# A hybrid decoder layer on one core: 32 of 152 attention steps turned by TensorE, and a written order for every engine in that stage

## The chip, the cores and the metric

The kernel runs on one core of one Trainium2 chip. The metric is the device time of one execution, in microseconds (us). The engines are TensorE (PE, with its weight load PEld), VectorE (DVE), ScalarE (ACT), GpSimd (POOL) and SyncE (SP). Before the change SP issues all DMAs. Each engine works through its own instructions in order, and waits where an operand is not ready.

## The reference, cut to what matters

```
a = rmsnorm(x, g_in)                                   # 2048 rows, 1024 wide
q, k, v, gate_b, u, v_a, gate_a = split(a @ w_in)      # 7 pieces of 512 columns
q, k = rope(rmsnorm(q)), rope(rmsnorm(k))              # 8 heads of 64
for (window, r) in ((128, 1), (512, 4), (2048, 16)):   # three dilated branches
    each block of 128 queries attends to its own and the previous 128 keys of its class
merge the three by their softmax denominators          # o_b
u, v_a = gelu(u), layernorm(gelu(v_a))                 # gMLP, chunks of 128 rows
o_a = u * (tril(w_spatial) @ v_a + b_spatial)          # 4 groups, 128 x 128 weights
h = x + [o_b * silu(gate_b), o_a * silu(gate_a)] @ w_out
out = h + sigmoid(rmsnorm(h) @ w_ple_gate + b) * (p @ w_ple_proj)
```

## The kernel before, in words

All large products are made of float32 words split in two parts, so a product of 128 rows by 512 columns is 24 matmuls (`project`, L223; `gm_product`, L640). Rows are worked in 16 tiles of 128.

Stage 1 computes q, k, v and gate_b tile by tile and writes them to DRAM (`d_qk`, `d_vp`, `d_vt`, `d_gb`). At its end PE's order is written by hand: g of tiles 14 and 15, q of both, k14, `spatial_weights` (L467), k15, v14, v15. `spatial_weights` masks the four 128 x 128 triangles on DVE (L476) and turns them on PE (L477); it needs the constants that `gm_constants` (L458) loads. In the same place three more groups of `w_in` columns (`va`, `ua`, `ga`) are loaded in pieces of 256 KB through four staging tiles named `raw` (L127), split by ACT (L133) and DVE or POOL (L135), and the first three quarters of q and k come back from DRAM (`load_qk`, L258).

Stage 2 is attention and gMLP together. Attention is a plan of 152 steps. A step has up to four segments of 128 or 256 keys. `scores` (L762) makes them on PE in a PSUM bank (`s` twice, `av` once in turn, L766), DVE adds the mask and takes the minimum (L773) and shifts it (L779), ACT takes the exponent (L781). `turn` (L784), one step later, makes two float16 words (ACT L788, POOL L789, which shows as L114), and one DMA transpose turns both (L792). `values` (L798), six steps after the scores, multiplies with v. Between `turn` and `values` PE gets a piece of gMLP: `fill(1.3)` (L821) takes some six of the 24 matmuls of a product. `gelu2` (L630), `gm_v`, `gm_u` and `gm_g` hold what follows such a product on ACT, DVE and POOL. Twelve groups of steps ("quads") make one pair of heads; the q and k of the next pair are loaded from the last quads of the pair before on (L848).

In stage 2 only PE's order is written (`manual_schedule(engines={PE})`, L533). The order of ACT, DVE, POOL and SP comes from the tile framework, which sets it from its own estimate of when each instruction can run.

Stage 3 (L866 on) finishes the last three gMLP chunks (`tail`), merges the branches, and does the output projection and the gate.

Of the kernel before, what the change touches and what calls it, by code (L numbers as in the profile page):

```python
# [10 lines left out]
F32 = mybir.dt.float32  # L11
F32R = mybir.dt.float32r
F16 = mybir.dt.float16
# [68 lines left out]
def hybrid_layer(ctx: ExitStack, tc: tile.TileContext, io, out):  # L82
# [11 lines left out]
    d_qk = [dram.tile([128, HEADS, S], F16, name=f"d_{n}") for n in "qk"]  # L94
# [151 lines left out]
    def gm_rows(c, pool):  # L246

        if c < NT and c not in GT:
            if c + 1 < NT:
                XT[c + 1] = load_x(d_at[c + 1])  # L250
            xt, aT = XT.pop(c), rows_T(pool)
            split_words(two(xt), aT)
            GT[c] = aT
# [4 lines left out]
    def load_qk(qk, hp, c, n=1):  # L258

        tl = slice(512 * c, 512 * (c + n))  # L260
        for h in range(2):
            nc.sync.dma_start(qk[0][h][:, tl], d_qk[0][:, 2 * hp + h, tl])
            yield
        for i in (0, 64):
            for t in range(2):
                nc.sync.dma_start(qk[1][i:i + 64, t, :, tl], d_qk[1][64 * t:64 * t + 64, 2 * hp:2 * hp + 2, tl])
            yield

    gating, s2 = ExitStack(), ExitStack()
    with ExitStack() as s1, ExitStack() as s1q:  # L270
# [156 lines left out]
        def turn_qk(n, which, hl):  # L427
# [8 lines left out]
            nc.sync.dma_start(d_qk[which][:, :, n * 128:(n + 1) * 128], st)  # L436
# [21 lines left out]
        def gm_constants():  # L458
            for name, src in (("lng", bcast(io["ln_v_g"], 512)), ("lnb", bcast(io["ln_v_b"], 512)),
# [5 lines left out]
                nc.sync.dma_start(dst if name != "gg" else dst.rearrange("p (g s) -> p g s", g=4), src)  # L465

        def spatial_weights():  # L467

            wsT, gg, bs = pg.tile([128, 4, 128], F32, name="wsT"), CG["gg"], CG["bs"]
            CG["wsT"] = wsT  # L470
            keep = stage()[:, 0:128]
            nc.vector.tensor_scalar(keep, CG["mask"][:, 384:512], 0.0, None, op0=OP.is_ge)
            pt = bank("pt", (128, 4, 128))
            for g in range(4):
                w = gg[:, g * 128:(g + 1) * 128]
                last = nc.vector.scalar_tensor_tensor(w, w, 0.25, keep, op0=OP.mult, op1=OP.mult)  # L476
                nc.tensor.transpose(pt[:, g], w, ident)  # L477
            nc.vector.tensor_copy(wsT, pt)
            with tc.issue_after(last.ins):
                nc.vector.tensor_scalar(bs, bs, 0.25, None, op0=OP.mult)  # L480
# [53 lines left out]
        for n in (NT - 2, NT - 1):  # L534
# [4 lines left out]
        qk = ([p2.tile([128, S], F16, name="sq" + n) for n in "01"],  # L539
              p2.tile([128, 2, 2, S], F16, name="sk"))  # L540
        gm_constants()
# [7 lines left out]
        load_gm("va", 5)  # L549
        for q in range(3):  # L550
            for _ in load_qk(qk, 0, q):
                pass
        step(NT - 2, "k")
        spatial_weights()
        step(NT - 1, "k")
        load_gm("ua", 4)
        step(NT - 2, "v")
# [66 lines left out]
    with s2:  # L624
# [4 lines left out]

        def gelu2(c, ps, name):  # L630
# [3 lines left out]
            nc.scalar.activation(t, ps, AF.Square, scale=math.sqrt(0.044715))  # L634
            nc.vector.scalar_tensor_tensor(t, t, 1.0, ps, op0=OP.add, op1=OP.mult)
            nc.scalar.activation(t, t, AF.Tanh, scale=math.sqrt(2 / math.pi))
            nc.vector.scalar_tensor_tensor(t, t, 1.0, ps, op0=OP.add, op1=OP.mult)  # L637
# [17 lines left out]
        def gm_v(c):  # L655
            ps = yield from gm_product(c, "va", {12: lambda: gm_rows(c + 1, stream)})
            t = gelu2(c, ps, "gv")
            st = small.tile([128, 6], F32, name="st")
            nc.vector.bn_stats(st, t)
            mv = small.tile([128, 2], F32, name="mv", bufs=2)  # L660
            nc.vector.bn_aggr(mv, st)
            rs = small.tile([128, 1], F32, name="rsl")
            rms_scale(rs, mv[:, 1:2], 1.0, 1, 4 * EPS)
            nc.vector.tensor_scalar(t, t, mv[:, 0:1], rs, op0=OP.subtract, op1=OP.mult)
            pool_tt(t, t, lng, OP.mult)
            pool_tt(t, t, lnb, OP.add)
# [5 lines left out]

        def gm_g(c):
            ps = yield from gm_product(c, "ga")
            GT.pop(c)
            t = pg.tile([128, 512], F32, name="gg")
            nc.scalar.activation(t, ps, AF.Tanh, scale=0.5)
# [291 lines left out]
```

## Time and profile before

| what | value |
| --- | --- |
| three runs | 1299.02, 1300.75 (median), 1304.36 us |
| profiled execution, its own time | 1296.61 us |
| its span, first to last instruction | 1294.8 us |
| busy share of the span: PE, DVE, ACT, POOL | 93%, 68%, 50%, 40% |
| mean granted TensorE clock | 0.979 of full speed |

A row of the timeline has the start, the length, the engine, the line, the operation, what is written from what, and how many instructions were merged; in brackets is the idle time before it and what ended that. A row of the stretches has the busy time of each engine, then the clock granted to PE (1.00 is full speed, 2.4 GHz), the mean share of the 16 DMA engines and GB/s. In the trace, the first attention scores start at 414.97 us and the last values end at 817.3 us.

### The profile page before, as it was taken

How to read it: one execution, taken by the hardware profiler on the slowest of the kernel's cores; microseconds unless marked ns; L12 is line 12 of the kernel's file. 1: busy time of each engine (PE TensorE's matmuls, PEld its weight loads, DVE VectorE, ACT ScalarE, POOL GpSimd, SP SyncE). 2: the span in 40 equal slices, each digit the busy share in tenths (PEclk: the TensorE clock that was granted, in tenths of full speed). 3: DMA queues.
4: the chain of work that ended last, by engine and by line, in shares of the span. 5: the costliest groups of instructions: out<-in, count | busy, mean ns of one | idle time of the engine just before them, and what ended most of it. 6: DMA issues, size and time to landing. Idle time of an engine off the chain costs nothing.

```text
span 1294.8 us, 21315 instructions
## 1 busy us (share of the span) xinstructions
PE 1198.9 (93%) x7166; PEld 972.6 (75%) x7166; DVE 878.0 (68%) x2253; ACT 647.6 (50%) x1273; POOL 516.2 (40%) x454
## 2 busy tenths in 40 slices
PE   5999999989949899899899899799999999999998
PEld 4778877777837687687687687677778888888887
DVE  5885665656546878678688679578866776666733
ACT  5754334343324677677677677144434434434422
POOL 4852444434334566556556556331312112121100
PEclk9999999999979999899999999899999999999999
DMA  7598776777679899999999999645454555654531
GB/s 260 160 230 199 178 185 155 167 181 179 163 198 241 198 207 220 220 233 222 222 222 222 221 226 211 179 135 186 119 168 119 156 168 131 153 159 127 143 90 49
DMA packets 442254, 233.21 MB, mean 180 GB/s; under 512 B 337440, under 2 KB 392864, under 8 KB 442144
## 3 DMA queue, kind: packets, MB, share of 16 engines
q1 hardware_dynamic: 442144, 231.85, 74.5%
q8 instruction: 56, 0.92, 0.3%
q14 instruction: 54, 0.44, 0.1%
HBM read 102.66 MB, written 57.28 MB: 124 GB/s over the span
## 4 chain that ended last, share of the span: by engine, by line
PE 40%; DMA 21%; DVE 14%; issue 7%; ACT 7%; POOL 6%; SPq 4%; DVEq 0%; ACTq 0%; POOLq 0%
PE mm L227 17%; PE mm L646 8%; PE gt L227 5%; DMA pt<-raw 4%; DMA st<-hl 4%; PE s L227 3%; DMA xt<-raw 3%; PE s L770 2%; PE pt L806 2%; DMA sk<-d_k 2%; ACT raw L179 2%; DVE aT L194 2%; DVE pr L773 2%; DVE m L421 1%; POOL rsh L148 1%
## 5 line engine op out<-in xcount | busy, mean ns | idle before, releaser
L227 PE MATMUL mm<-wslot,aT 128*128 128x512 f32 x1536 | 361.6, 391 | 5.8 <-ACT wslot L133 3.3
L227 PEld LDWEIGHTS mm<-wslot,aT 128*128 128x128 f32 x1536 | 288.5, 188 | 68.4 <-ACT wslot L133 4.6
L646 PE MATMUL mm<-wslot,aT 128*128 128x512 f32 x1152 | 312.5, 412 | 2.9 <-DVE gv L637 2.4
L646 PEld LDWEIGHTS mm<-wslot,aT 128*128 128x128 f32 x1152 | 210.1, 194 | 42.0 <-DVE gv L637 3.0
L114 POOL TENSOR_TENSOR raw<-pr,raw 128x512 f16<-128x512 f32 (+1 forms) x152 | 178.9, 1183 | 136.2 <-ACT raw L788 114.1
L781 ACT ACTIVATE pr<-pr,ost 128x256 f32<-128x256 f32 (+1 forms) x384 | 150.3, 451 | 67.4 <-DVE ost L779 66.3
L227 PE MATMUL gt<-wslot,aT 128*128 128x512 f32 x744 | 179.0, 395 | 4.0 <-DVE gb L453 3.5
L227 PEld LDWEIGHTS gt<-wslot,aT 128*128 128x128 f32 x744 | 140.7, 190 | 36.6 <-DVE gb L453 5.2
L806 PEld LDWEIGHTS <-pt 128*128 128x128 f16 x1800 | 65.2, 98 | 65.2 <-DMA pt<-raw 32.6
L788 ACT ACTIVATE raw<-pr 128x512 f16<-128x512 f32 (+1 forms) x152 | 93.0, 619 | 34.9 <-DMA pt<-raw 32.9
L806 PE MATMUL pt<-sv,pt 128*128 128x65 f16 x1800 | 83.1, 195 | 24.5 <-DMA pt<-raw 23.3
L773 DVE CUSTOM_DVE_ANT_0 pr<-s,mask 128x256 f32<-128x256 f32 (+1 forms) x256 | 80.9, 360 | 24.6 <-POOL raw L114 11.8
L227 PE MATMUL s<-wslot,aT 128*128 128x512 f32 x384 | 91.9, 395 | 1.4 <-POOL wslot L135 1.4
L227 PE MATMUL av<-wslot,aT 128*128 128x512 f32 x360 | 86.8, 395 | 6.3 <-DVE gb L453 5.3
L114 POOL TENSOR_TENSOR m<-m,m 128x512 f32<-128x512 f32 x32 | 48.1, 1503 | 98.5 <-DVE rsh L147 92.6
L227 PEld LDWEIGHTS s<-wslot,aT 128*128 128x128 f32 x384 | 73.2, 191 | 17.2 <-POOL wslot L135 1.8
L227 PEld LDWEIGHTS av<-wslot,aT 128*128 128x128 f32 x360 | 67.5, 189 | 22.8 <-DVE gb L453 7.0
L770 PEld LDWEIGHTS <-sq 128*128 128x128 f16 x768 | 70.3, 121 | 16.7 <-issue 12.8
L582 POOL TENSOR_TENSOR ob<-ob 128x512 f32<-128x512 f32 x16 | 21.0, 1310 | 143.3 <-DVE ob L580 143.3
L770 PE MATMUL s<-sk,sq 128*128 128x256 f16 (+1 forms) x512 | 73.7, 279 | 4.1 <-DMA sk<-d_k 2.0
L585 POOL TENSOR_TENSOR ma<-ob,ma 128x512 f32<-128x512 f32 x16 | 23.7, 1483 | 121.7 <-DMA ma<-d_gb 86.4
L779 DVE TENSOR_SCALAR ost<-ost 128x2 f32<-128x2 f32 (+1 forms) x152 | 63.1, 417 | 2.3
(198 smaller groups left out, 1722.1 us busy)
## 6 DMA issues: line engine op xcount, KB each, us to landing
xt<-x SPq DMA_DIRECT2D x32, 512.0 KB, 4.4
d_o<-ost SPq DMA_DIRECT2D x48, 264.0 KB, 3.5
raw<-w_in SPq DMA_DIRECT2D x38, 256.0 KB, 3.8
sv<-d_vt SPq DMA_DIRECT2D x32, 264.0 KB, 3.6
ob<-d_o SPq DMA_DIRECT2D x16, 528.0 KB, 4.5
xt<-d_at SPq DMA_DIRECT2D x16, 512.0 KB, 4.4
out<-th SPq DMA_DIRECT2D x32, 256.0 KB, 2.7
d_at<-raw SPq DMA_DIRECT2D x28, 256.0 KB, 2.5
```

What stands on the lines that cost most here:

```text
L114: nc.gpsimd.tensor_tensor(dst, a, b, op=op)
L179: nc.scalar.activation(turned[t].bitcast(U16), words[:, t], AF.Copy)
L194: nc.vector.tensor_tensor(lo, f, hi.bitcast(F32), op=OP.subtract)
L227: nc.tensor.matmul(ps, aT[:, ha, k, :], w(slot, hw, k), start=(n == 0), stop=(n == 3 * nk - 1))
L585: nc.gpsimd.tensor_tensor(m, o, m, op=OP.mult)
L646: nc.tensor.matmul(ps, GT[c][:, ha, k, :], slots[g][:, hw, k, :], start=(n == 0), stop=(n == 23))
L770: nc.tensor.matmul(ps[:, c:c + nk], cols(br, j, Q[h]), cols(br, j, K, n, h, self.nb), start=(n == 0), stop=(n == 1))
L773: nc.vector.tensor_tensor_reduce(pr[:, c:c + nk], ps[:, c:c + nk], mask[:, m - nk:m], -1.0, 3e38, op0=OP.add, op1=OP.min, accum_out=o[:, j ...
L779: nc.vector.tensor_scalar(nm, nm, math.log(PSCALE), None, op0=OP.add)
L781: nc.scalar.activation(pr[:, c:c + nk], pr[:, c:c + nk], AF.Exp, bias=o[:, j - j0, 130 + h:131 + h], scale=-1.0)
L788: nc.scalar.activation(ph, pr[:, :width], AF.Copy)
L806: nc.tensor.matmul(PO[0][:, j % 2, h], self.pt[:, t, c // 128], vt[:, h, vv, 0:65], start=(n == 0), stop=(n == 3 * self.nb - 1))
```

## The change

Names are as in the code above. What is changed:

- The triangles are masked later (`spatial_scales`), and turned on PE (`spatial_weights`) only when the first `gm_g` starts, inside stage 2.
- The constants, and the first three quarters of q and k, are issued by ACT. q and k in DRAM are laid out by quarters, so that a quarter is three DMAs (before six), with 2 KB runs.
- In stage 2 every engine's order is written: `manual_schedule()` for all. `later(n, ...)` puts gMLP's follow-up operations n steps on; the loop says what stands where in a step.
- In steps whose `j` is odd, in the last two and first two quads of each pair of heads (32 of 152), `turn_on_pe` takes the place of the two words, the POOL subtraction and the DMA transpose: two steps later PE turns the float32 weights in four 128 x 128 pieces into bank `av`, ACT copies the high word out, and DVE subtracts to make the low one. Scores use only the two `s` banks.
- The v tiles are issued by ACT, behind a step's exponents.
- `fill` is also called in the last seven turns of the loop, and the copy of finished values (`out`) stands one turn later.

```
-    d_qk = [dram.tile([128, HEADS, S], F16, name=f"d_{n}") for n in "qk"]
+    d_qk = [dram.tile([128, 4, HEADS, 512], F16, name=f"d_{n}") for n in "qk"]
...
+    def load_qk(qk, hp, c, eng=nc.sync):
+        hs = slice(2 * hp, 2 * hp + 2)
+        eng.dma_start(qk[0][:, :, 512 * c:512 * c + 512], d_qk[0][:, c, hs])
+        yield
+        src = d_qk[1][0:64, c, hs]
         for i in (0, 64):
+            eng.dma_start(qk[1][i:i + 64, c].rearrange("p t h s -> p t (h s)"),
+                          bass.AP(tensor=src.tensor, offset=src.offset,
+                                  ap=[[4 * HEADS * 512, 64], [64 * 4 * HEADS * 512, 2], [1, 1024]]))
+        yield
...
-                nc.sync.dma_start(dst if name != "gg" else dst.rearrange("p (g s) -> p g s", g=4), src)
+                nc.scalar.dma_start(dst if name != "gg" else dst.rearrange("p (g s) -> p g s", g=4), src)
...
         load_gm("va", 5)
+        gm_constants()
+        step(NT - 2, "k")
         for q in range(3):
-            for _ in load_qk(qk, 0, q):
+            for _ in load_qk(qk, 0, q, nc.scalar):
                 pass
-        step(NT - 2, "k")
-        spatial_weights()
         step(NT - 1, "k")
         load_gm("ua", 4)
+        spatial_scales()
...
+            later(1, lambda: nc.scalar.activation(t, ps, AF.Square, scale=math.sqrt(0.044715)))
+            later(2, lambda: nc.vector.scalar_tensor_tensor(t, t, 1.0, ps, op0=OP.add, op1=OP.mult),
+                  lambda: nc.scalar.activation(t, t, AF.Tanh, scale=math.sqrt(2 / math.pi)))
+            later(3, lambda: nc.vector.scalar_tensor_tensor(t, t, 1.0, ps, op0=OP.add, op1=OP.mult))
...
+        def spatial_weights():
+            wsT = CG["wsT"] = pg.tile([128, 4, 128], F32, name="wsT")
+            ps = bank("gt", (128, 4, 128))
+            for g in range(4):
+                nc.tensor.transpose(ps[:, g], CG["gg"][:, g * 128:(g + 1) * 128], ident)
+            nc.vector.tensor_copy(wsT, ps)
...
-            nc.sync.dma_start(t, rows)
+            nc.scalar.dma_start(t, rows)
             V[br, j0] = t
...
-                ps = bank("s" if self.tick % 3 else "av")
+                ps = bank("s")
...
+            def turn_on_pe(self):
+                ps = bank("av", (128, 4, 128))
+                for k in range(4):
+                    nc.tensor.transpose(ps[:, k], self.pr[:, k * 128:(k + 1) * 128], ident)
+                self.pt = pt = p2b.tile([128, 8, 128], F16, name="pt", bufs=PH) \
+                    .rearrange("p (t k) q -> p t k q", t=2)
+                nc.scalar.activation(pt[:, 0], ps, AF.Copy)
+                nc.vector.tensor_tensor(pt[:, 1], ps, pt[:, 0], op=OP.subtract)
...
-        with in_order:
+        with in_order, tc.manual_schedule():
...
+            for n in range(len(plan) + LAG_C + 1):
+                now[0] = n
...
+                    steps[n].scores()
+                if 0 <= n - LAG_C - 1:
+                    steps[n - LAG_C - 1].out()
+                    steps[n - LAG_C - 1] = None
+                if 2 <= n < len(plan) + 2 and steps[n - 2].on_pe:
+                    steps[n - 2].turn_on_pe()
+                for f in due.pop(n, ()):
+                    f()
+                if n < len(plan):
+                    steps[n].exps()
+                    steps[n].on_pe = i % 12 in (10, 11, 0, 1) and j % 2 == 1 and steps[n].width == 512
+                    if not steps[n].on_pe:
+                        steps[n].high()
...
+                if 0 <= n - LAG_B < len(plan) and not steps[n - LAG_B].on_pe:
                     steps[n - LAG_B].turn()
-                    fill(FILL)
-                if 0 <= n - LAG_C:
+                if n < len(plan) and not steps[n].on_pe:
+                    steps[n].low()
+                fill(FILL)
+                if 0 <= n - LAG_C < len(plan):
                     steps[n - LAG_C].values()
```

PE at the end of stage 1, before the change (`pt`, `mm`, `s`, `av`, `gt` are PSUM banks; the rows are g, q, k14, the triangles, k15, v14, v15 and the first gMLP product):

```order
L227 MATMUL pt<-wslot,aT 128x512 x48
L227 MATMUL mm<-wslot,aT 128x512 x48
L227 MATMUL s<-wslot,aT 128x512 x24
L477 MATMUL pt<-ident,gg 128x128 x4
L227 MATMUL s<-wslot,aT 128x512 x24
L227 MATMUL av<-wslot,aT 128x512 x24
L227 MATMUL gt<-wslot,aT 128x512 x24
L646 MATMUL mm<-wslot,aT 128x512 x28
```

The same place on PE after the change:

```order
L228 MATMUL pt<-wslot,aT 128x512 x48
L228 MATMUL mm<-wslot,aT 128x512 x48
L228 MATMUL s<-wslot,aT 128x512 x48
L228 MATMUL av<-wslot,aT 128x512 x24
L228 MATMUL gt<-wslot,aT 128x512 x24
L654 MATMUL mm<-wslot,aT 128x512 x28
```

The four transposes of the triangles have left this place; they stand in the fourth step's turn of the attention loop now.

SP in the same place before, from the gate tiles on (`raw` are pieces of `w_in`, `sq` and `sk` the q and k that come back, `st` a transpose of fresh q or k):

```order
L454 DMA d_gb<-gb 128x512 x2
L465 DMA lng<-ln_v_g 128x512
L465 DMA lnb<-ln_v_b 128x512
L465 DMA mask<-c_mask 128x512
L465 DMA bs<-b_spatial 128x4x1
L465 DMA gg<-w_spatial 128x4x128
L262 DMA sq_3090<-d_q 128x512
L262 DMA sq_3091<-d_q 128x512
L266 DMA sk<-d_k 64x2x512 x4
...
L127 DMA raw<-w_in 128x512
```

SP there after the change:

```order
L457 DMA d_gb<-gb 128x512 x2
L128 DMA raw<-w_in 128x512 x4
L433 DMA_TRANSPOSE st<-hl 128x8x128
L128 DMA raw<-w_in 128x512 x2
L439 DMA d_q<-st 128x8x128
L128 DMA raw<-w_in 128x512 x2
L433 DMA_TRANSPOSE st<-hl 128x8x128
```

The constants and the q and k loads stand on ACT now, and the pieces of `w_in` follow the gate tiles at once, with the transposes of fresh q among them.

DVE in two steps at the start of the second pair of heads, before (`pr` are the weights, `ost` the minimum and the finished values):

```order
L773 ISA pr,ost<-s,mask 128x256
L773 ISA ost 128x1
L773 ISA pr,ost<-s,mask 128x256
L773 ISA ost 128x1
L779 TENSOR_SCALAR ost<-ost 128x2
L812 COPY ost<-pt 128x2x130
L773 ISA pr,ost<-av,mask 128x256
L773 ISA ost 128x1
L773 ISA pr,ost<-av,mask 128x256
L773 ISA ost 128x1
L635 SCALAR_TENSOR_TENSOR gu<-gu,mm 128x512
L779 TENSOR_SCALAR ost<-ost 128x2
```

DVE in two steps of the same stretch after the change (`pt<-av,pt` is the subtraction of `turn_on_pe`):

```order
L803 ISA pr,ost<-s,mask 128x256
L803 ISA ost 128x1
L803 ISA pr,ost<-s,mask 128x256
L803 ISA ost 128x1
L809 TENSOR_SCALAR ost<-ost 128x2
L822 TENSOR_TENSOR pt<-av,pt 128x512
L803 ISA pr,ost<-s,mask 128x256
L803 ISA ost 128x1
L803 ISA pr,ost<-s,mask 128x256
L803 ISA ost 128x1
L809 TENSOR_SCALAR ost<-ost 128x2
L852 COPY ost<-pt 128x2x130
```

Every second step the subtraction stands ahead of the step's own masking, and the minimum's shift always follows its step's masking directly.

## Rows read from the trace of the kernel before

**Rows 1.** Stretch around the loads of the second pair of heads.

```profile
520.00:560.00 40.00, 35.42 (x316) 27.40 (x313) 28.10 (x106) 26.22 (x56) 24.82 (x21) 0.91 1.12 227
```

**Rows 2.** Timeline of PE from k14 to the third attention step.

```profile
363.54 5.60 PE L227 MATMUL s<-wslot,aT 128*128 128x512 f32 x24
389.80 1.09 PE L477 MATMUL pt<-ident,gg 128*128 128x128 f32 x4 [20.66 <-DVE gg L476]
390.54 7.36 PE L227 MATMUL s<-wslot,aT 128*128 128x512 f32 x24
...
414.97 0.40 PE L770 MATMUL av<-sk,sq 128*128 128x128 f16 x4
...
424.31 0.64 PE L770 MATMUL av<-sk,sq 128*128 128x256 f16 x4 [4.82 <-DVE ost L773]
```

**Rows 3.** PE's waits from 415 to 817 us: total us, times, longest.

```profile
PE pt L806 <- DMA pt<-raw: 23.3, 17, 4.5
...
PE s L770 <- DVE ost L773: 0.3, 1, 0.3
```

**Rows 4.** Three stretches without PE idle; below, the values' matmuls alone.

```profile
546.00:610.00 64.00, 64.00 (x657) 52.71 (x655) 50.83 (x214) 48.14 (x112) 38.77 (x34) 1.00 1.03 226
640.00:690.00 50.00, 50.00 (x505) 40.96 (x504) 41.68 (x176) 37.90 (x91) 29.84 (x27) 1.00 1.05 223
740.00:800.00 60.00, 60.00 (x610) 49.49 (x607) 49.34 (x208) 45.68 (x106) 37.62 (x34) 1.00 1.04 216
...
420.00:820.00 400.00, 83.12 (x1800) 65.25 (x1800) 0.97 1.04 220
546.00:610.00 64.00, 15.06 (x336) 11.83 (x334) 1.00 1.03 226
640.00:690.00 50.00, 11.39 (x252) 8.93 (x252) 1.00 1.05 223
740.00:800.00 60.00, 13.78 (x307) 10.78 (x303) 1.00 1.04 216
```

**Rows 5.** DMA issues from 440 to 800 us: count, median us to landing.

```profile
pt<-raw SPq DMA_TRANSPOSE x145, 4.0
```

**Rows 6.** SP, DVE and ACT around the pieces of w_in, end of stage 1.

```profile
376.39 0.68 DVE L424 TENSOR_TENSOR hl<-m,hl 128x512 f16<-128x512 f32 x1
...
382.13 1.29 SPq L430 DMA_TRANSPOSE st<-hl  x1
...
388.18 2.48 SPq L127 DMA_DIRECT2D raw<-w_in  x4
...
423.83 0.63 ACT L133 ACTIVATE wslot<-raw 128x512 fp32r<-128x512 f32 x1 [0.79 <-DMA raw<-w_in]
```

**Rows 7.** PE at the last values and at transposes of stage 3.

```profile
809.06 0.54 PE L806 MATMUL pt<-sv,pt 128*128 128x65 f16 x12 [2.82 <-DMA pt<-raw]
...
816.50 0.84 PE L806 MATMUL pt<-sv,pt 128*128 128x65 f16 x12 [4.51 <-DMA pt<-raw]
817.15 10.09 PE L646 MATMUL mm<-wslot,aT 128*128 128x512 f32 x36
...
879.49 0.60 PE L155 MATMUL av<-ident,ma 128*128 128x128 f32 x4
879.85 5.84 PE L646 MATMUL mm<-wslot,aT 128*128 128x512 f32 x24
```

**Rows 8.** ACT and DVE after such transposes; then attention's forms: busy us, mean ns.

```profile
874.60 0.58 ACT L157 ACTIVATE aT<-av 128x512 fp32r<-128x512 f32 x1
...
875.35 0.68 DVE L158 TENSOR_TENSOR aT<-av,aT 128x512 fp32r<-128x512 f32 x1
...
L781 ACT ACTIVATE pr<-pr,ost 128x256 f32<-128x256 f32 x216 | 97.1, 499 | 44.3 <-DVE ost L779 43.2 <-DVE rsl L147 0.5 <-DVE mv L661 0.3
...
L779 DVE TENSOR_SCALAR ost<-ost 128x2 f32<-128x2 f32 x112 | 50.6, 452 | 1.8
...
L773 DVE CUSTOM_DVE_ANT_0 pr<-s,mask 128x256 f32<-128x256 f32 x144 | 55.0, 418 | 13.3 <-POOL raw L114 6.9 <-PE s L770 4.7 <-issue 1.1
```

## What the change will do to the time, predicted blind

> **What bounds the kernel now.** I read the page first: PE is busy 93% of the span, so what PE waits for is nearly all there is to win. The chain of waits and the stretches then show where the other 7% lies. After 930 us PE runs almost without a break, and nothing of the change is there. Two places are left.
>
> The first is the end of stage 1. The timeline of PE shows 20.66 us of idle ahead of the four triangle transposes, because the masked triangles come late from DVE; the product behind them then takes 7.36 us where its twin took 5.60 [rows 2]. A wait of 4.82 us follows at the third attention step, whose bank DVE has not emptied.
>
> The second is attention. Three stretches of it, 174 us together, have no idle PE at all. They hold 895 of the 1800 matmuls of `values`, so 75.6 of 152 steps, or 2.30 us a step [rows 4]. At that rate 152 steps take 350 us, and the values of the last six steps about 2 more. The stage takes from 414.97 [rows 2] to 816.50 + 0.84 [rows 7], 402.4 us: 50 us over. PE's waits in it add up to 35.7 us in eight kinds, of which the first is 23.3 for turned weights that a DMA has not delivered [rows 3]; the other 15 us are reduced clock and small gaps. They sit where the next pair of heads is loaded: from 520 to 560 us the clock is 0.91, and the DMA engines are at 1.12 [rows 1]. The reader is to see that these DMA engines are full throughout attention (1.03 to 1.05 even where PE never waits), so any extra load shows as late weights.
>
> **Part by part.**
>
> *Triangles later.* The 20.66 us wait and the 1.8 us of the slowed product go; with the 4.82 us behind, 27.3 us can be won. What is late next are the pieces of `w_in`. In before, 16 of them (ua, ga) are issued from 388.18, and ACT splits the last at 423.83 + 0.63 [rows 6]: 2.26 us each. In the new order of DVE the first masking stands behind 13 of the 16. The first of them is issued behind the transpose of q14, whose operand DVE finished at 376.39 + 0.68, while SP reached that transpose only at 382.13 for the loads ahead of it [rows 6], which are on ACT now. So 377.1 + 0.4 + 13 x 2.26 = 407. PE would want the third step's bank at 424.31 - 4.82 - 20.66 - 1.8 = 397 [rows 2]. I take a new wait of 10 us: 17.3 won. The bounds are 27.3 (the pieces come faster with SP free) and 0 (they come no sooner than before). That ACT now issues 14 loads in this place, ahead of its own splits, speaks for the lower half.
>
> *32 steps turned by PE.* Added on PE: 128 transposes of 128 x 128 float32, in fours. Four of the same kind took 0.36 us from start to the next product's start [rows 7]; 32 x 0.36 = 11.5, and I take 12. The bounds are 11.5 and 32 x 0.74 = 24, which is the four triangles' time to the next product at the lowered clock [rows 2]. Added on ACT: nothing, a copy of 0.58 us from PSUM [rows 8] replaces a copy. Added on DVE: 32 x 0.68 = 22 us [rows 8]. Removed: 32 POOL subtractions, which nothing waits long for, and 32 DMA transposes out of 152, that is a fifth of what fills the DMA engines in the worst places.
>
> The Trainium skill (VectorE: DVE Perf Modes, "The three transpose paths") gives 390 ns for a 128 x 128 transpose on TensorE, of 16-bit words. The trace has four float32 ones in 0.36 us when they follow each other [rows 7], so it disagrees. By the page, as an estimate, 128 of them would cost 50 us, and the sum would come out 38 us higher.
>
> *The written order.* Does DVE keep up? In the full-rate stretches DVE is busy 141.9 us for 75.6 steps, 1.88 us a step, and ACT 1.74 [rows 4]. A pair of steps with one turn on PE needs 2 x 1.88 + 0.68 = 4.4 us of DVE, and PE needs 2 x 2.30 + 0.36 = 5.0. It fits, at 90%. But there is a ring: transposes 0.60 [rows 7], ACT's copy 0.58, DVE's subtraction 0.68, two maskings 0.84, the shift 0.45, two exponents 1.00 [rows 8], and then the next transposes may start. That is 4.15 us of the 5.0, and five hand-overs and gMLP's operations between must fit in the rest. So I count 0.3 us of PE wait for each of the 32, 9.6 us, and 5 us for reduced clock and the rest of the stage: 15 us of waits stay of the 50 - 4.8 = 45.6, and 30.6 go. The bounds are 0 (all stay) and 45.6 (none).
>
> *The end of attention.* The four waits of 2.82 to 4.51 us in the last six steps [rows 7] are in the 23.3 already. `fill` now covers them with the 36 product matmuls that stood behind, so these cost nothing twice.
>
> *v by ACT, loads by quarters, two banks for scores.* I count these at zero. 48 issues of v at 0.62 us, the time of a `w_in` issue [rows 6], are 30 us of ACT, 0.2 a step, beside 1.74 busy of 2.30. Where an issue waits for PE to release a v tile, the next step's exponents queue behind it on ACT, and the weights of that step are due only six steps later. If that cover is gone, the price is in the slower rival. With two banks, scores wait if DVE is two steps behind, which the 90% above decides.
>
> *Stage 3* starts with less work in hand, as 36 matmuls went ahead: I add 2 us (bounds -3 and 6, of waits of that size there).
>
> Sum on the profiled execution, 1296.6 us: -17.3 - 30.6 + 12 + 2 = -33.9, which is 1262.7. The median of the runs is 4.1 us above it, so I forecast 1267 us.
>
> **The rivals.**
>
> *PE never waits.* The pieces of `w_in` come in time and the ring has slack: -27.3 - 45.6 + 12, so 1240 us. For it: the DMA load falls where it was worst. Against it: the ring is nearly as long as its pair of steps.
>
> *The head's gain is eaten by the `w_in` pieces.* 17.3 us less: 1284 us. For it: 2.26 us a piece held over 16 pieces. Against it: the same queue had 18 q and k loads in between.
>
> *The waits stay.* Turning 32 steps relieves nothing that PE waits for, the turned weights are as late as ever: 30.6 us less gained, 1297 us, no change. Against it: half the steps of the bad stretches no longer depend on a DMA, and a turn has 4.0 us median landing [rows 5] against six steps of 2.30.
>
> *Transposes at the page's price.* 38 us more than in the forecast, 1305 us, by the Trainium skill's figure named above; the row of four stands against it.
>
> *Slower: the written order binds DVE.* If DVE, at the head of whose line stands a subtraction that waits for ACT and PE, falls behind, the two `s` banks pass that to PE in every step. The sum breaks even when the waits come to 15 + 33.9 = 49 us, 0.32 us for each of 152 steps. At 0.45 us a step, 68 us, the time is 1320 us. For it: in before, the order was set with the actual readiness in view, and DVE's other inputs (POOL's and ACT's results) come with varying delay. Against it: DVE is 82% busy in the full-rate stretches (1.88 of 2.30) and never stops PE there.
>
> **How the numbers follow.** Forecast 0.56, its own range 1252 to 1282; PE never waits 0.18; head eaten 0.09; waits stay 0.06; page's price 0.02; slower 0.09. A run of this kernel can tell 0.5%, 6.5 us, from no change. The first three are faster: 0.83. The next two are the same: 0.08. Slower 0.09. The range for 8 in 10 reaches from 1243, close to the case without waits, to 1296, short of the case where they stay.
>
> **What would show it.** Right: no wait at the triangles; k15's product directly after k14's, in 5.4 to 5.6 us; a wait near 10 us at the third step, ended by DVE; a mean step near 2.40 us over the stage; four `ident,pr` transposes in about 0.36 us; waits for turned weights down from 23.3 to a few us, and none over 1 us at the end of the stage. Wrong: waits of `s` for DVE in most steps outside the loads, a DVE over 95% busy, PE idle over 20 us before the third step, or over 0.6 us for four transposes.

## The result, and the profile after

The changed kernel takes 1361.24 us (median of four runs, 1358.48 to 1366.20), the kernel before 1299.88 in the same session. The ratio is 1.0477, 95% interval 1.0453 to 1.0502. It is slower, where I forecast 1267 us and faster.

Stage by stage, in the profiled executions (1366.20 us, the slowest of the four, and 1296.61 before), the first scores start at 409.97 us (before: 414.97 [rows 2]), 5 us earlier, and the last values end near 892.2 (before: 817.3 [rows 7]), 75 us later; after them both kernels need about the same (472 us in after, 477 before). So attention takes 482.2 us instead of 402.4, and all that was lost was lost there. Its two lines among the stretches, of before first (columns: stretch, length, busy us and instructions of PE, PEld, DVE, ACT and POOL, granted clock, DMA share, GB/s):

```profile
414.97:817.34 402.37, 366.44 (x3538) 293.45 (x3538) 306.99 (x1208) 282.63 (x631) 239.55 (x205) 0.97 1.04 221
```

The same of after:

```profile
409.97:892.19 482.22, 410.36 (x3714) 322.82 (x3714) 317.79 (x1247) 296.00 (x640) 195.94 (x174) 0.95 0.75 171
```

PE is idle 71.9 us (482.22 - 410.36) where it was idle 35.9. The share of the DMA engines falls from 1.04 to 0.75. Part of that is only the longer stage: share times length falls from 418 to 362 us, by 14%. So the relief came, and it did not help. PE is busy 43.9 us more, for 128 transposes, 36 product matmuls that stood behind attention before and 12 smaller ones, and for work at a lower clock (0.95).

What PE waits for in this stretch of after (waited for: us in total, times, longest):

```profile
PE s L795 <- DVE ost L803: 39.0, 34, 6.7
PE s L795 <- DMA sq<-d_q: 19.4, 6, 5.9
PE av L818 <- ACT pr L811: 7.4, 14, 3.0
PE mm L654 <- DVE gv L645: 5.6, 4, 3.0
```

Of the 23.3 us for turned weights [rows 3] nothing is left. Two kinds stand in their place: scores that wait for DVE to empty their bank (5.6 us before, 4.82 of them at the third step), and scores that wait for a load of q (none before). Neither comes from DVE being full; it is busy 318 of 482 us. The largest waits of DVE itself say why the first kind exists (whole span):

```profile
DVE pt L822 <- ACT pt L821: 74.1, 30, 4.4
...
DVE aT L195 <- ACT aT L194: 34.3, 19, 3.4
```

L822 is the subtraction of a step turned on PE, L195 DVE's half of the split of the gMLP rows. Both wait for ACT at the head of DVE's written line, and maskings stand behind them. One turn of this ring, DVE in the timeline of after (start, length; L809 is the shift):

```profile
547.42 0.73 DVE L809 TENSOR_SCALAR ost<-ost 128x2 f32<-128x2 f32 x1
550.27 0.69 DVE L822 TENSOR_TENSOR pt<-av,pt 128x512 f16<-128x512 f32 x1 [2.13 <-ACT pt L821]
550.88 0.41 DVE L803 CUSTOM_DVE_ANT_0 pr<-s,mask 128x256 f32<-128x256 f32 x1
...
551.68 0.92 DVE L809 TENSOR_SCALAR ost<-ost 128x2 f32<-128x2 f32 x1
552.51 0.41 DVE L852 COPY ost<-pt 128x260 f32<-128x260 f32 x1
552.85 0.67 DVE L643 SCALAR_TENSOR_TENSOR gu<-gu,mm 128x512 f32<-128x512 f32 x1
...
554.24 0.17 DVE L809 TENSOR_SCALAR ost<-ost 128x2 f32<-128x2 f32 x1
```

And ACT and PE beside it:

```profile
548.18 0.91 ACT L811 ACTIVATE pr<-pr,ost 128x256 f32<-128x256 f32 x2 [0.99 <-DVE ost L809]
549.12 0.63 ACT L826 ACTIVATE raw<-pr 128x512 f16<-128x512 f32 x1
549.66 0.58 ACT L821 ACTIVATE pt<-av 128x512 f16<-128x512 f32 x1
...
549.29 0.60 PE L795 MATMUL s<-sk,sq 128*128 128x256 f16 x4
```

Read it as a circle: the shift of one step lets ACT do its exponents and its copy to raw; behind those on ACT stands the copy of the turned step; that lets DVE subtract; and only then come the next step's masking and shift, out's copy, a gelu operation, and the masking and shift of the step after. From shift to shift of two steps that is 554.24 - 547.42 = 6.8 us. The masking at 550.88 was held up: its scores were done at 549.89 (549.29 + 0.60), while DVE stood idle. The turn is a usual one; from the first to the last of the eight subtractions around it, seven turns, pass 45.7 us, 6.5 each:

```profile
522.67 0.69 DVE L822 TENSOR_TENSOR pt<-av,pt 128x512 f16<-128x512 f32 x1 [4.36 <-ACT pt L821]
...
568.39 0.69 DVE L822 TENSOR_TENSOR pt<-av,pt 128x512 f16<-128x512 f32 x1 [2.12 <-ACT pt L821]
```

PE could do a pair in 5: its own rate where it doesn't wait is the same as before, 2.2 us a step:

```profile
503.56 0.61 PE L795 MATMUL s<-sk,sq 128*128 128x256 f16 x4
...
505.79 0.61 PE L795 MATMUL s<-sk,sq 128*128 128x256 f16 x4
```

The Trainium skill (Trainium Architecture — The Big Picture, "Inside one NeuronCore") says that each engine has an instruction stream of its own and meets the others only through semaphores. The trace agrees, and shows the price of one such meeting: 2.13 us of DVE at 550.27, with the masking that empties PE's bank right behind.

The other wait is seen where SP and PE are laid side by side. SP in after:

```profile
512.18 0.53 SPq L263 DMA_DIRECT2D sq<-d_q  x1
```

PE there:

```profile
509.83 0.54 PE L843 MATMUL pt<-sv,pt 128*128 128x65 f16 x12
516.13 1.04 PE L795 MATMUL s<-sk,sq 128*128 128x256 f16 x4 [5.75 <-DMA sq<-d_q]
```

The load brings the first quarter of the next pair of heads. It is written into the program one step ahead of these scores, which belong to the third quad of a branch and read other quarters; the step that reads it comes six steps later. Yet PE waits until it has landed, and runs at the lower clock behind (1.04 us for scores of 0.60).

Stage 1's end, PE in after (its counterpart is [rows 2]):

```profile
363.81 11.04 PE L228 MATMUL s<-wslot,aT 128*128 128x512 f32 x48
...
380.13 5.60 PE L228 MATMUL gt<-wslot,aT 128*128 128x512 f32 x24
401.49 8.63 PE L654 MATMUL mm<-wslot,aT 128*128 128x512 f32 x28 [15.77 <-ACT aT L194]
...
420.77 1.01 PE L795 MATMUL s<-sk,sq 128*128 128x256 f16 x4 [6.66 <-DVE ost L803]
```

The triangles' wait is gone, and k15's product follows k14's at once (48 matmuls in 11.04 us); 15.77 and 6.66 us of waits have come for 20.66 and 4.82.

### The profile page after: what moved, and what is told of

It reads as the page before. It is cut to its first block, busy times and chain, and to the rows that moved or that the text cites. A ratio compares the mean times of both kernels' runs of the same rounds, so it can differ in the third digit from the quotient of the medians.

```text
span 1364.4 us, 21385 instructions
## 1 busy us (share of the span) xinstructions
PE 1231.6 (90%) x7294; PEld 993.2 (73%) x7294; DVE 888.3 (65%) x2285; ACT 656.0 (48%) x1273; POOL 472.9 (35%) x422
## 4 chain that ended last, share of the span: by engine, by line
PE 37%; DVE 15%; ACT 7%; DMA 5%; issue 4%; SPq 1%; POOL 1%; ACTq 0%; DVEq 0%; POOLq 0%
PE mm L228 16%; PE mm L654 7%; PE gt L228 5%; DVE pr L803 4%; PE s L795 3%; PE s L228 3%; ACT pr L811 2%; PE pt L843 2%; ACT raw L826 2%; DVE ost L809 1%; DVE wslot L136 1%; DMA ob<-d_o 1%; DVE pt L822 1%; ACT pt L821 1%; DVE aT L195 1%
## 5 line engine op out<-in xcount | busy, mean ns | idle before, releaser
L228 PE MATMUL mm<-wslot,aT 128*128 128x512 f32 x1536 | 362.9, 391 | 7.6 <-ACT aT L194 3.2
L654 PE MATMUL mm<-wslot,aT 128*128 128x512 f32 x1152 | 320.7, 418 | 27.7 <-ACT aT L194 15.8
L115 POOL TENSOR_TENSOR raw<-pr,raw 128x512 f16<-128x512 f32 (+1 forms) x120 | 137.9, 1149 | 237.4 <-ACT raw L826 160.5
L795 PE MATMUL s<-sk,sq 128*128 128x256 f16 (+1 forms) x768 | 112.1, 283 | 58.5 <-DVE ost L803 39.0
L803 DVE CUSTOM_DVE_ANT_0 pr<-s,mask 128x256 f32<-128x256 f32 (+1 forms) x384 | 120.8, 359 | 28.5 <-PE s L795 25.3
L795 PEld LDWEIGHTS <-sq 128*128 128x128 f16 x768 | 73.8, 122 | 67.3 <-issue 44.5
L228 PEld LDWEIGHTS s<-wslot,aT 128*128 128x128 f32 x384 | 71.9, 188 | 17.3 <-POOL wslot L136 2.2
L826 ACT ACTIVATE raw<-pr 128x512 f16<-128x512 f32 (+1 forms) x120 | 74.9, 624 | 3.9
L822 DVE TENSOR_TENSOR pt<-av,pt 128x512 f16<-128x512 f32 x32 | 22.1, 692 | 76.4 <-ACT pt L821 74.1
```

Source lines behind the costliest of these rows:

```text
L115: nc.gpsimd.tensor_tensor(dst, a, b, op=op)
L228: nc.tensor.matmul(ps, aT[:, ha, k, :], w(slot, hw, k), start=(n == 0), stop=(n == 3 * nk - 1))
L654: nc.tensor.matmul(ps, GT[c][:, ha, k, :], slots[g][:, hw, k, :], start=(n == 0), stop=(n == 23))
L795: nc.tensor.matmul(ps[:, c:c + nk], cols(br, j, Q[:, h]), cols(br, j, K, n, h, self.nb), start=(n == 0), stop=(n == 1))
L803: nc.vector.tensor_tensor_reduce(pr[:, c:c + nk], ps[:, c:c + nk], mask[:, m - nk:m], -1.0, 3e38, op0=OP.add, op1=OP.min, accum_out=o[:, j ...
L822: nc.vector.tensor_tensor(pt[:, 1], ps, pt[:, 0], op=OP.subtract)
```

## The experiments

Each was timed in rounds beside the kernel before, whose median in the four sessions was 1301.2 to 1302.0 us. All but h1 start from the changed kernel (1361.2). Differences are of medians, mostly from different sessions; the ratios with their 95% intervals are to the kernel before in the same session. Waits are read from one profiled execution of each.

**e1: no step on the PE.**

```
- steps[n].on_pe = i % 12 in (10, 11, 0, 1) and j % 2 == 1 and steps[n].width == 512
+ steps[n].on_pe = False
```

> The changed kernel, but no step is turned by the PE: all 152 go through ACT, POOL and the DMA transpose. Theory P (the steps on the PE form a ring over DVE and ACT): the trace of the changed kernel has 19 us of waits of the scores for DVE in the stretches with steps on the PE, 7.4 us of transposes that wait for the exponents, and about 0.6 us each for 32 times four transposes, 19 us. These 45 us go, and of the 23.3 us of waits for turned weights of the kernel before all or none come back: 1316 to 1340 us. Theory O (the written order itself is the loss, whatever turns the weights): DVE still binds, the transposes by DMA are late again, and the time stays between 1350 and 1375 us.

1329.4 us (ratio 1.0212, 1.0192 to 1.0233): 32 us less, as theory P has it. In this order, then, the 32 steps cost more than they relieve. No wait for turned weights over 1 us in sum came back, PE's waits for DVE fell from 39.0 to 22.5 us, and the waits for sq grew to 34.3.

**e2: two tiles for sq.**

```
- qk = (p2.tile([128, 2, S], F16, name="sq"), ...
+ qk = ([p2.tile([128, S], F16, name="sq" + n) for n in "01"], ...
- eng.dma_start(qk[0][:, :, 512 * c:512 * c + 512], d_qk[0][:, c, hs])
+ for h in range(2): eng.dma_start(qk[0][h][:, 512 * c:512 * c + 512], d_qk[0][:, c, 2 * hp + h])
```

> The changed kernel, but sq is two tiles again, one for each head, each loaded by its own DMA. Theory F (a false wait): in the changed kernel a quarter of both heads is loaded by one DMA into one tile, the quarters of the two heads lie 2048 columns apart, and what lies between is taken as written too; so the scores of the very next step wait for a load that they don't read, 19.4 us in six waits, and the clock falls behind each. These waits go, with 0 to 10 us of reduced clock behind them: 1332 to 1342 us. Theory L (the loads are late because SP issues them behind transposes that wait for POOL): the scores that wait are those that read the quarter, two tiles change nothing, 1356 to 1366 us.

1341.1 us (1.0307, 1.0284 to 1.0331), 20 us less. No wait for sq is left among PE's waits:

```profile
PE s L796 <- DVE ost L804: 44.9, 38, 9.3
PE mm L655 <- ACT aT L194: 15.7, 1, 15.7
```

So the wait was false: a write to two strips of one tile was taken to cover what lies between them. Of its 19.4 us, 6 came back as waits of the scores for DVE (44.9 for 39.0) and a few more at other places. That the gain is 20 us all the same is in part the clock: the mean granted clock of the profiled execution rose from 0.972 to 0.977, some 6 us of 1342 as an estimate.

**e3: the subtraction behind the masking and shift.**

```
- nc.vector.tensor_tensor(pt[:, 1], ps, pt[:, 0], op=OP.subtract)      # in turn_on_pe
+ def low_on_pe(self):
+     nc.vector.tensor_tensor(self.pt[:, 1], self.words, self.pt[:, 0], op=OP.subtract)
...
  steps[n].exps()                                                       # masking, shift, exponents
+ if 2 <= n < len(plan) + 2 and steps[n - 2].on_pe:
+     steps[n - 2].low_on_pe()
```

> The changed kernel, but of a step turned by the PE the subtraction on DVE stands behind the masking and shift of the step two later, not ahead of them; the transposes and ACT's copy stay in place. Theory P: the subtraction holds DVE until ACT's copy, 74 us in 30 waits, and the maskings behind it hold the two banks of scores; with it behind, most of the 19 us of PE's waits for DVE in these stretches go, and DVE's wait at the subtraction falls below 20 us: 1335 to 1352 us. Rival B (two banks are too few in any order): PE's waits for DVE stay near 39 us, 1355 to 1366 us.

1335.1 us (1.0271, 1.0239 to 1.0303), 26 us less: theory P. PE's waits for DVE fell from 39.0 to 29.2, those of the transposes for the exponents from 7.4 to 0.2; the rest of the gain is spread and not seen in PE's waits. DVE's wait at the subtraction fell from 74 to 13.7 us, and its wait at the split of the rows rose from 34 to 59: the next one in line.

**i1: the split of the gMLP rows, DVE's half one step later.**

```
- later(1 + 2 * i, lambda i=i, part=part: split_words((part,), aT[:, :, 4 * i:4 * i + 4]))
+ f, d = part.rearrange("p (k t) -> p k t", t=128), aT[:, :, 4 * i:4 * i + 4]
+ later(1 + 2 * i, lambda f=f, d=d: nc.scalar.activation(d[:, 0], f, AF.Copy))
+ later(2 + 2 * i, lambda f=f, d=d: nc.vector.tensor_tensor(d[:, 1], f, d[:, 0].bitcast(F32), op=OP.subtract))
```

> The changed kernel with DVE's half of the gMLP rows' split one step later than ACT's, and nothing else. After the other two edits this gave 32 us. Theory P (it is a loss of its own, 34 us of DVE's waits in 18 places): it gives 15 us or more by itself, 1330 to 1346 us. Rival S (both waits stand in one line, and while the subtraction holds DVE, the split's wait is hidden): 1350 to 1362 us.

1343.0 us (1.0331, 1.0283 to 1.0379), 18 us less: a loss of its own. PE's waits for DVE fell from 39.0 to 25.6 us.

**e8 and e10: two edits, three edits.**

> The changed kernel with two tiles for sq and with the subtraction behind the masking and shift, the two edits that alone gave 20 and 26 us. Theory P (two separate losses): they add, 1361 - 20 - 26 = 1315, so 1310 to 1320 us. Rival (where PE waits for the load DVE catches up, so that without that wait its own shows): 1322 to 1332 us.

> As with two tiles for sq and the subtraction behind the masking; besides, DVE's half of the split of the gMLP rows is written one step later than ACT's half. With the subtraction behind the masking DVE waits 59 us in 27 places at this split for ACT, ahead of maskings. Theory P (whatever stands at the head of DVE's line and waits for ACT costs PE time): 8 to 16 us less than with the two edits, 1300 to 1308 us. Rival (DVE has that time to spare where PE is not bound by it): within 4 us of the two edits.

e8: 1314.6 us (1.0106, 1.0076 to 1.0135); the two add (1361 - 20 - 26 = 1315). e10, with i1's edit as well: 1282.8 us (0.9860, 0.9826 to 0.9895), faster than the kernel before. The third edit gave 32 us, twice the most that I expected and 14 more than alone. That one wait at the head of DVE's line hides what the next would cost fits this; it is not shown further. What PE waits for in attention in e10:

```profile
PE s L798 <- DVE ost L806: 13.0, 11, 7.8
PE gt L706 <- POOL gv L115: 2.2, 1, 2.2
PE mm L657 <- DVE gv L648: 1.8, 3, 0.9
PE av L821 <- ACT pr L814: 1.1, 3, 0.6
```

That is 18 us for 71 in after, and 7.8 of it is the one wait at the third step. DVE itself still waits 27.6 us at the subtraction, but the step's masking and shift now stand ahead of it. Seven turns of the ring take 35.4 us, 5.05 each, as PE needs:

```profile
502.16 0.69 DVE L828 TENSOR_TENSOR pt<-av,pt 128x512 f16<-128x512 f32 x1 [1.25 <-ACT pt L824]
...
537.51 0.69 DVE L828 TENSOR_TENSOR pt<-av,pt 128x512 f16<-128x512 f32 x1 [1.24 <-ACT pt L824]
```

The attention of e10 takes 405.3 us, 3 more than before, but it holds the 128 transposes and the 36 product matmuls besides. Its line among the stretches:

```profile
405.56:810.86 405.30, 387.18 (x3714) 312.01 (x3714) 327.30 (x1246) 293.36 (x639) 196.19 (x174) 0.98 0.92 202
```

A step turned on PE in e10, in PE's timeline, where nothing waits:

```profile
534.00 0.60 PE L798 MATMUL s<-sk,sq 128*128 128x256 f16 x4
534.43 0.60 PE L821 MATMUL av<-ident,pr 128*128 128x128 f32 x4
534.79 1.63 PE L657 MATMUL mm<-wslot,aT 128*128 128x512 f32 x6
536.26 0.54 PE L849 MATMUL pt<-sv,pt 128*128 128x65 f16 x12
536.64 0.60 PE L798 MATMUL s<-sk,sq 128*128 128x256 f16 x4
...
538.86 0.60 PE L798 MATMUL s<-sk,sq 128*128 128x256 f16 x4
539.21 1.64 PE L657 MATMUL mm<-wslot,aT 128*128 128x512 f32 x6
```

The scores' start to the product's start is 0.79 us with the four transposes and 0.35 without (538.86 to 539.21): 0.44 for four, 14 us for 32.

**e5 and e12: no written order for the engines other than PE.**

```
- with in_order, tc.manual_schedule():
+ with in_order:
```

> The changed kernel with a written order for the PE alone, as in the kernel before; ACT, DVE, POOL and SP are ordered by the scheduler from the same program. Theory O (instructions at the head of a written line wait while ready ones stand behind them): DVE's waits at the subtraction and at the split of the gMLP rows shrink from 74 and 34 us to under 20 each, PE's waits for DVE from 39 to under 15, and the false waits for sq stay: 1315 to 1335 us. Rival B (two banks for scores, and the steps on the PE themselves, cost the time in any order of the others): PE's waits for DVE stay over 30 us, 1350 to 1366 us.

> The changed kernel with a written order for the PE alone and with two tiles for sq. Theory F: the 23 us of false waits go from the 1310 us of the free order: 1284 to 1292 us, so that the scheduler's order of ACT, DVE, POOL and SP and the mended written order (1283 us) are worth the same. Rival (behind the false waits stand others, of DVE): 1297 to 1308 us.

e5: 1309.8 us (1.0067, 1.0046 to 1.0089), 51 us less, more than I expected; DVE's waits at the two places are 3.7 and 0.2 us, and PE's waits for DVE 11.0, of which 10.4 is one wait. e12, with two tiles as well: 1290.9 us (0.9911, 0.9883 to 0.9938). So the scheduler, from the same program, had put other work of DVE ahead of those two. The mended written order is 8 us better than the scheduler's by the medians; their intervals overlap a little.

**e9, e11 and i3: what the steps on the PE are worth, and the third bank.** e9 is e2 and e1 together, e11 is e10 without steps on the PE, and i3 is e11 with

```
- ps = bank("s")
+ ps = bank("s" if self.tick % 3 else "av")
```

> The changed kernel with two tiles for sq and with no step turned by the PE. With no step on the PE alone the trace has 34.3 us of waits for sq and none for turned weights. Theory F (these waits are false and cover nothing): they go, 1329 - 34 = 1295, so 1293 to 1303 us. Rival D (they gave the DMA transposes time, and the turned weights are late without them, as in the kernel before, 23 us): 1308 to 1320 us.

> As e10 (two tiles for sq, DVE's half of the split one step later), but with no step turned by the PE. Asked is what the 32 steps on the PE buy once nothing else holds DVE. Theory N (nothing): the PE's 32 x 0.6 us of transposes, 20 us, go, and 10 to 23 us of waits for turned weights come back, as with two tiles and no step on the PE and as in the kernel before: 1273 to 1288 us. Rival (the DMA engines are full without them, and waits for weights bring a lower clock too): 1290 to 1305 us.

> As e11 (two tiles for sq, the split one step later, no step on the PE), but the scores have three banks again, as in the kernel before, since no transposes need the third. Theory 3 (with two banks the PE is tied to DVE two steps back): most of e11's 19.9 us of waits for DVE go, and 8 to 15 us of time: 1285 to 1292 us. Rival (the waits stand where DVE itself is late, at the head and at the loads): 1295 to 1303 us.

e9: 1312.7 us (1.0095, 1.0061 to 1.0130), not the 1295 that theory F had from the false waits alone: 10.1 us of waits for turned weights and 15 us more of waits for DVE took half of it. e11: 1299.9 us (0.9987, 0.9970 to 1.0003), 17 us slower than with the steps on the PE. Theory N (they buy nothing) is wrong. In it PE waits in attention for

```profile
PE pt L846 <- DMA pt<-raw: 20.0, 16, 5.4
PE s L798 <- DVE ost L806: 19.9, 16, 9.8
```

So the steps on the PE lose 32 us in the order as changed and win 17 once DVE's line is mended. i3: 1296.8 us (0.9953, 0.9925 to 0.9980), 3 us from e11 with overlapping runs (1289 to 1301, and 1295 to 1305). PE's waits for DVE did fall, from 19.9 to 6.8 us, but not the time by the 8 to 15 us of theory 3; without steps on the PE a third bank is worth little at best.

**i2: v issued by SP again**, on e10 (`nc.scalar.dma_start(t, rows)` to `nc.sync`).

> As e10, but the 48 loads of v are issued by SP again. I had counted this part of the change at zero. Theory Z: 1279 to 1287 us. Rival Q (on SP a load of v stands in the written line behind transposes that wait for POOL, and holds those behind it while it waits for a free v tile): 1290 to 1305 us.

1286.7 us (0.9886, 0.9844 to 0.9928) beside 1282.8: zero within what the runs can tell (1282.6 to 1288.9, and 1281.8 to 1285.2).

**e4, h1, h2 and i4: the end of stage 1.** e4 puts the constants and first q and k loads back on SP. h1 is the kernel before with the triangles later and nothing else. h2 is e10 with every second piece of w_in for the gMLP staged in pr; i4 is h2 with the second and third quarter of q and k loaded after the pieces:

```
- slots[g] = load_group(w_in, 512 * c, new_slot(), stage, WD2)
+ def stage_gm():                                                       # h2
+     turn[0] += 1
+     return stage() if turn[0] % 2 else p2.tile([128, 512], F32, name="pr", bufs=PR)
+ slots[g] = load_group(w_in, 512 * c, new_slot(), stage_gm, WD2)
...
- for q in range(3): ... load_qk(qk, 0, q, nc.scalar)
+ for _ in load_qk(qk, 0, 0, nc.scalar): ...                            # i4; 1, 2 and 3 on SP, ahead of the loop
```

> The changed kernel, but the five constants and the first nine loads of q and k are issued by SP again, at the same places of the program. Theory A (ACT's issues hold the splits of w_in): in the changed kernel ACT issues nothing else from 368.75 to 376.72 us but these loads, and the wait of 15.8 us ahead of the first gMLP product follows from pieces that are split late; the wait falls by 5 to 12 us, 1349 to 1357 us. Rival W (the pieces are bound by their four buffers and by what stands in order with them on DVE and POOL): the wait stays within 3 us of 15.8, 1358 to 1366 us.

> The kernel before with one part of the change alone: the masked triangles are turned by the PE at the first gate product instead of ahead of k15's product. Theory W (the end of stage 1 is set by the pieces of w_in, whatever PE does meanwhile): the wait of 20.7 us goes, and waits of about the same sum stand ahead of the first gMLP product and of the third step, as in the changed kernel (15.8 and 6.7): 1294 to 1304 us. Rival G (the gain that I predicted): 17 us less, 1280 to 1288 us.

> As e10, but every second piece of w_in for the gMLP is staged in the three buffers of pr, which are idle then, besides the four of raw. Theory R (a round trip through four buffers): a piece holds a buffer for a landing of 4.2 us, ACT's and DVE's or POOL's split and the wait in SP's line, four of them give the 2.26 us a piece; with seven the last piece is split 8 us sooner or more, and the waits of 12.7 and 7.8 us in e10 shrink with it: 1266 to 1276 us. Rival D (the DMA engines are full, busy share near 1 from 370 to 424 us): the pieces come no sooner, 1278 to 1288 us.

> As with seven staging buffers, but of the q and k loads at the end of stage 1 only the first quarter stays there; the second and third, 1.5 MB, are issued by SP after the pieces of w_in, with the fourth. Theory D (the end of stage 1 is bound by what the DMA engines can carry, about 240 KB a microsecond there): the pieces come about 6 us earlier, the two waits of 12.0 and 5.9 us shrink by 4 to 8 us, and the time is 1272 to 1277 us. Rival L (the quarters then come too late for the fourth to eighth steps, or hold the first transposes in SP's line): 1280 to 1292 us.

e4: 1363.8 us (1.0473, 1.0447 to 1.0499), no change; its wait ahead of the first gMLP product is 15.9 us. That ACT's queue was taken by 14 loads was not the cause. h1: 1293.2 us (0.9931, 0.9912 to 0.9951), 8 us of the 17 that I had counted (6 to 11 by the interval). In the two profiled executions it is 4 us ahead at the first values (429.81, before 433.86). In h1 PE waits in place of the triangles for

```profile
PE mm L641 <- ACT aT L193: 11.5, 1, 11.5
PE av L774 <- DVE ost L777: 7.5, 1, 7.5
```

These 19 us are what 25.5 became when the triangles stood in nobody's way.

h2: 1280.2 us (0.9831, 0.9813 to 0.9850); three more buffers bring 3 us by the medians, with overlapping intervals, where a round trip through four buffers would have given 6 or more. The waits are 12.0 and 5.9, for 12.7 and 7.8 in e10. i4: 1277.7 us (0.9821, 0.9784 to 0.9858); 1.5 MB less ahead of the pieces brings 2.5 us more by the medians and 1.3 by the ratios, which is not clear of the noise, and less than the 4 to 8 expected:

```profile
PE mm L661 <- ACT aT L255: 10.8, 1, 10.8
PE s L802 <- DVE ost L810: 5.1, 1, 5.1
```

Neither the buffers, nor ACT's queue, nor 1.5 MB of loads alone sets the end of stage 1. What does is open. From 370 to 420 us the share of the DMA engines is 1.00 in after, 1.01 in h2 and still 1.03 in i4, so that they are full is a rival that no run removed. i4 has the lowest median, 1.8% under the kernel before (1.4 to 2.2).

## Why the prediction was wrong

**The step that failed is the written order.** The ring that I put at "4.15 us of the 5.0" takes 6.8 us in the turn shown and 6.5 on the average, so it does not fit beside PE's 5.0. I had closed it over the turned step alone. But ACT's copy of a turned step stands behind the next step's exponents and its copy to raw; these wait for that step's shift, and the shift stands on DVE behind its own maskings and behind the subtraction before them. So the ring runs through the other step, from shift to shift: a shift 0.45, two exponents 1.00, the copy to raw 0.62, ACT's copy 0.58, the subtraction 0.68, two maskings 0.84, a shift 0.45 and two maskings 0.84. That is 5.5 us; with out's copy (0.41) and a gelu operation (0.67) in the same line it is 6.5. The transposes and the turned step's own exponents, which I had counted, are not links of it. The prices of the 5.5 us stood in [rows 8] and in the page of before (0.62 is the mean of L788). What I wrote "must fit in the rest" I did not add up. e3 shows it: the same work with the subtraction behind the masking and the shift, 26 us.

The second such place, the split of the gMLP rows, is missing from my sum altogether (18 us alone in i1, 32 behind the others in e10). Busy shares could not show either, since DVE was never full: the loss is waiting at the head of a line.

This was my slower rival, with its mechanism named. I gave it 0.09 and, at 68 us of waits, 1320 us; the kernel is 41 us slower still, 20 of them false waits that the rival did not have. What I set against it, that DVE "never stops PE there", was a statement about the scheduler's order, set from the framework's own estimate (not "with the actual readiness in view"), and the change took it away. e5 shows that the written order of the other four engines alone was worth 51 us.

The kernel is 94 us above the forecast. The two places on DVE are 26 and 32 of them, the false waits 20, and 16 are left in e10.

**Loads by quarters, counted at zero, cost 20 us** (e2). I looked at who issues them, and not at what the new tile makes overlap.

**v by ACT and two banks, counted at zero**, are zero within what the runs can tell (i2, i3), the banks only without steps on the PE.

**32 steps on PE**: the transposes were priced right. 0.44 us for four in e10 makes 14 us; I took 12, with a bound of 24. The 390 ns each of the Trainium skill (VectorE: DVE Perf Modes, "The three transpose paths"), 50 us in all as an estimate, does not hold here. The relief was right too, but after can't show it: e1, with no step on the PE, has no waits for turned weights to speak of either, probably because PE is late there for other reasons. With DVE's line mended there are none with the 32 steps (e10) and 20.0 us without (e11).

**Triangles later**: the mechanism was right (the pieces of w_in are late next), the size was not: 8 us by the medians of h1 where I took 17.3. In the changed kernel the waits at that place add up to 22.4 us beside 25.5 before, and by the first values it was 8 us behind (441.78, before 433.86). I had set a wait at the third step only; the larger one stands ahead of the first gMLP product, whose rows ACT splits behind pieces that it waits for.

**Stage 3**: I added 2 us. What follows the last values is 5 us shorter, but the 36 product matmuls (10 us in [rows 7]) are now done earlier, inside attention. Without them it is some 5 us longer, an estimate, and inside my bounds of -3 to 6.

With the failed step and the false waits mended the total comes out at 1282.8 us in e10: inside the 1243 to 1296 that I gave, and 16 us above the forecast, of which the triangles are 9. PE waits 18 us in its attention, 7.8 of them at the third step, where I had counted 15, with reduced clock, and 10.

Of the signs that I had named for right, three came: no wait at the triangles, k15's product directly behind k14's, and four transposes in 0.36 us where nothing waits (534.43 to 534.79 in e10). Of those for wrong, one came (PE idle up to the third step, 15.8 + 6.7, over 20 us). The waits of `s` for DVE came in 34 of 152 steps, not in most, and DVE was far from 95% busy: I had looked for a full engine, and it was a waiting one.

## What to carry to other kernels

Before writing an engine's order by hand, list for each instruction in it that waits for another engine what stands behind it, and follow the circle until it closes over every engine's line, all links added; a busy share of 66% says nothing about this. Place the consumer of a hand-over behind work that is ready (e3), or one step later than its producer (i1): moving two instructions on DVE gave 58 of the 78 us between the changed kernel and e10. And when two tiles become one, check what a strided write to it is taken to cover.

## What was not expected of the hardware

- Four 128 x 128 float32 transposes on PE between other matmuls took 0.44 us more than none (e10), 0.11 us each.
- Two waits cost more than their length. In after, behind the false wait at 516.13 and behind the one at 420.77, the granted clock was at the lower of its two levels (columns as above; the first row is the wait itself):

```profile
509.90:516.10 6.20, 0.47 (x13) 0.35 (x12) 1.93 (x8) 2.36 (x5) 2.08 (x2) 0.91 1.02 239
516.10:520.20 4.10, 4.07 (x26) 3.65 (x27) 0.95 (x5) 1.54 (x3) 0.16 (x1) 0.50 0.76 212
...
420.70:426.80 6.10, 5.27 (x19) 3.66 (x19) 4.68 (x17) 4.75 (x11) 1.02 (x2) 0.50 0.99 218
```

At full rate the work of 516.10 to 520.20 would have taken about half of its 4.1 us: as an estimate, 2 us more for a wait of 5.75.
